# A two-layer decoder trunk on one core: x rows, early products and subtractions between the layers

## The chip, the cores and the metric

The kernel runs on one core of one Trainium2 chip. Its time is the device time of one execution in microseconds. The kernel before was timed in three runs: the median is 1912.34 us, the lowest 1910.25, the highest 1913.97. The engines named below are TensorE (PE, matmuls; PEld its weight loads), VectorE (DVE), ScalarE (ACT), GpSimd (POOL) and SyncE (SP), which issues all the transfers that matter here.

## What is computed

A trunk of two layers over 1024 rows of width 1024. Each layer adds the normalised result of a mixer to x; layer 0 mixes by a gated MLP, layer 1 by dilated attention.

```python
for i in range(DEPTH):                 # DEPTH = 2
    h = rms_norm(x, norm_pre[i])
    if i % 2 == 0:
        y = gmlp_mixer(h, ...)         # ends with y @ w_out
    else:
        y = dilated_attention_mixer(h, ...)   # begins with h @ w_in: q, k, v of 3 groups, and z
    x = x + rms_norm(y, norm_post[i])
```

All is float32. The change lies between the end of the first layer (`y @ w_out`, the addition to x) and the beginning of the second (`rms_norm` and `h @ w_in`).

## The kernel before

**Products.** Each float32 operand is split into a high and a low part (`split`: a cast on ScalarE, a subtraction on VectorE, names with hi/lo, h/l), and each product step is three matmuls (`mm3`, lines 82 to 84). The projections of layer B go by Strassen's scheme: the activations (operands `b_hi`/`b_lo` 1 to 7) and the weights (`whi`/`wlo` 1 to 7) are added up to seven pairs, and seven products of half size take the place of eight. A `Chunk` is one such projection: bv00 is the values of the first group and heads, bqk000 and bqk001 are two of queries and keys. One product is 12 matmuls of 128x512. Products 1 and 2 need no sums, only the plain upper row half's operands and one plain quarter of the weight. The weights of a chunk come in four loads (`wb0`, `wb2`, `wb1`, `wb3`, 256 KB each) into a ring of five buffers ("wraw"); four sums on POOL (`sums`, line 90) make the others: t1 from b12 and b11, t2 from b22 and t1, b12 anew, and t4. A later chunk's load goes into a buffer only when its earlier reader is done.

**The end of layer A.** `wout_unit` multiplies by w_out (accumulators `po`): loads `wr` and `yr`, their splits `oh`/`ol` and `yh`/`yl`, 16 steps. Row tiles 0, 1, 4, 5 are done first, then `post` of these four, then 2, 3, 6, 7, and `post(6)` and `post(7)` last. `post(t)` is a chain: mean square `ms_pa` on VectorE, its power −1/2 `rstd_pa` on POOL (line 105), x loaded to `xr`, `xr` = yt·rstd + xr in two halves on VectorE (line 580), stored to `x1d`; then the same norm for layer B: squares `jk_b` on ScalarE, `ms_b`, `rstd_b` on POOL, `yt` = xr·rstd·g1b in two halves on VectorE (line 154). Then the rows are brought into operands: `put_top` for tiles 0 to 3, and for 4 to 7 `put_rest`, which makes a sum and three differences with the rows of the tile 4 below, one difference on VectorE and two on POOL. Each operand is four transposes on TensorE (`pt_b`, line 128), a cast on ScalarE and a subtraction on VectorE. `yt` and `xr` share one ring "wk" of nine buffers.

**What sets the order.** Each engine runs its own queue in order. Up to the first products of layer B a scheduler sets the order by priorities and its own estimate of times; behind these the order of TensorE is written out: `in_turn` makes a list of tasks (chunk, product), `pipeline` loads weights ahead, and `drive` goes through the list and puts attention work, entered with `later(work, wait)`, between the matmuls after so many ticks (a tick is one step of three matmuls). The attention's first matmuls are the scores `s` (line 765) from K and Q, which come by 16 transfers out of the tiles `b_c`. The accumulators have tags: "mm" three banks, "o" one bank.

Of the kernel before, what the change touches and what calls it, by code (L numbers as in the profile page):

```python
# [15 lines left out]
P = 128  # L16
# [8 lines left out]
WAIT = 16  # L25
SOON = 300
SLOW = 4
RATE3 = 0.16
# [5 lines left out]
def trunk_kernel(  # L34
# [99 lines left out]

    def put_rest(pool, ops, h0, h1, t, name, first):

        a11, a12, a21, a22 = h0[:, 0:512], h0[:, 512:1024], h1[:, 0:512], h1[:, 512:1024]
        s1 = pool.tile([P, 512], F32, tag="sums", bufs=2, name=f"sums_{name}")
        add(s1, a21, a22)
        sub(a21, a11, a21, first)  # L140
        sub(a11, s1, a11, nc.gpsimd)
        sub(a12, a12, a11, nc.gpsimd)
        for i, a in ((4, a22), (5, s1), (7, a21), (6, a11), (3, a12)):
            put_op(ops, i, a, t, name)
# [133 lines left out]
    def in_turn(chunks, early=False, banks=5):  # L278

        out, n = [], 0
        if early:
            a, b = chunks[:2]
            out = [(a, 1), (a, 2), (b, 1), (b, 2), (a, 6), (a, 5), (a, 7), (b, 6), (a, 4)]
            out += [(a, 3), (b, 5), (b, 7)] if banks == 3 else [(b, 5), (a, 3), (b, 7)]
            n = 2
        for c, last in zip(chunks[n:], [chunks[n - 1] if n else None, *chunks[n:]]):
            if banks == 3:
                out += [(c, 1), (last, 4), (last, 3), (c, 6), (c, 2), (c, 5), (c, 7)]  # L290
            else:
                out += [(c, 1), (last, 4), (c, 2), (last, 3), (c, 6), (c, 5), (c, 7)]
        out += [(chunks[-1], 4), (chunks[-1], 3)]
        return [(c, i) for c, i in out if c]
# [237 lines left out]

    WK = 9
    bops = new_ops("b")
    with ExitStack() as octx:
        op = octx.enter_context(tc.tile_pool(name="op", bufs=1, reuse_waits="tile"))
        gpb = op.tile([P, D], F32, name="gpb")
        nc.sync.dma_start(out=gpb, in_=gpost[0].partition_broadcast(P))
        g1b = op.tile([P, D], F32, name="g1b")
        nc.sync.dma_start(out=g1b, in_=gpre[1].partition_broadcast(P))  # L540
# [3 lines left out]
        def wout_unit(tiles, dh):  # L544
# [6 lines left out]
            for t in tiles:  # L551
                turn[0] = (turn[0] + 1) % 4
                po[t] = psum("mm" if turn[0] else "o", [P, 512], f"po_{dh}_{t}")
                if t not in yts:
                    yts[t] = op.tile([P, D], F32, tag="wk", bufs=WK, name=f"yt_{t}")
                    sq2[t] = op.tile([P, 2], F32, tag="sq2", bufs=8, name=f"sq2_{t}")
# [18 lines left out]
        def post(t):  # L575
            r = rstd_of(op, sq2[t], f"pa_{t}")
            xt = op.tile([P, D], F32, tag="wk", bufs=WK, name=f"xr_{t}")
            nc.sync.dma_start(out=xt, in_=x[t * P:(t + 1) * P, :])
            for hs_ in HALVES:
# [6 lines left out]
            else:  # L586
                put_rest(op, bops, hs[t - 4], hs[t], t - 4, f"b{t - 4}", nc.vector)

# [71 lines left out]
    def v_chunk(q, g):  # L660
# [20 lines left out]

        return proj_t(wb[q * 10 + g * 3], bops, newb, f"bv{q}{g}", lambda th, ct, o: None, out=out, done=done)

    def qk_chunk(q, g, pr):
# [23 lines left out]
        def done():  # L708
            later(lambda: attention(q, g, pr), WAIT)
            if (q, g, pr) == (3, 2, 1):  # L710
                rate[0] = RATE3

        return proj_t(wb[q * 10 + g * 3 + 1 + pr], bops, newb, f"bqk{nm}", qk_out, done=done)

    def z_chunk(q):
# [13 lines left out]

        return proj_t(wb[q * 10 + 9], bops, newb, f"bz{q}", z_out, hooks={i: lambda c=c: prep(c) for c, i in enumerate((2, 5, 7, 4))} if q == 3 else None)  # L730

    merged, through = set(), set()
# [220 lines left out]
    side = deque()  # L953
    credit, rate = [0.5], [RATE]
    now = [0]
# [72 lines left out]
    tasks = in_turn(chunks, True, 3)  # L1028
    run(pipeline(tasks[:4], 3, tasks[4:]))
    with tc.manual_schedule(engines={mybir.EngineType.PE}):  # L1030
        drive(pipeline(tasks[4:], 3))

# [146 lines left out]
```

## Time and profile before

| | |
|---|---|
| median of three runs | 1912.34 us |
| the profiled execution's own time | 1916.06 us |
| its span, first to last instruction | 1914.3 us |
| mean granted clock of TensorE | 0.987 |
| busy: PE / DVE / ACT / POOL | 1836.5 / 1302.0 / 1002.8 / 486.1 us |
| DMA | 242.22 MB, mean 127 GB/s |

Times in the rows below are in us from the span's start. The change touches the stretch from about 620 to 820 us. Layer A's out projection ends at 739, layer B's products run from there to the end.

### The profile page before, as it was taken

The page shows a single profiled execution, that of the slowest core. Times are in us where ns is not written, and L with a number is a line of the kernel's source. Part 1 is how long each engine was busy: PE and PEld are TensorE (multiplying, and loading weights), DVE is VectorE, ACT ScalarE, POOL GpSimd, SP SyncE. Part 2 cuts the span into 40 slices and gives each one's busy share as a digit, 9 for nine tenths or more (in the row PEclk, how much of TensorE's full clock was granted, in tenths as well). Part 3 has the DMA queues.
Part 4 walks back from the last instruction along what each step waited for, and adds up shares of the span by engine and source line. Part 5 has one row for each costly group of instructions (what it writes and reads, how often), then busy time and mean ns, then how long its engine had stood idle before and what let it go on. Part 6 is the DMA issues. An engine that isn't in the chain of part 4 may idle for free.

```text
span 1914.3 us, 29722 instructions
## 1 busy us (share of the span) xinstructions
PE 1836.5 (96%) x10024; PEld 1507.9 (79%) x10024; DVE 1302.0 (68%) x2530; ACT 1002.8 (52%) x2280; POOL 486.1 (25%) x359
## 2 busy tenths in 40 slices
PE   6899999999999897999999999999999999999998
PEld 6899888888888675777778777788777787778777
DVE  6855766576555877558587685669684866868583
ACT  6544455555644665355554457464556444555931
POOL 3331343443300204222213123321233221222100
PEclk9999999999999999999999999999999998999999
DMA  6242433433256575232233554334644335433873
GB/s 209 87 129 82 140 123 114 138 118 96 78 186 232 164 248 183 67 84 74 80 82 88 156 146 119 71 86 125 165 107 105 78 90 156 130 85 74 247 208 110
DMA packets 231847, 242.22 MB, mean 127 GB/s; under 512 B 98448, under 2 KB 150288, under 8 KB 231696
## 3 DMA queue, kind: packets, MB, share of 16 engines
q1 hardware_dynamic: 231696, 240.34, 43.4%
q8 instruction: 79, 1.29, 0.3%
q14 instruction: 72, 0.59, 0.1%
HBM read 170.46 MB, written 44.63 MB: 112 GB/s over the span
## 4 chain that ended last, share of the span: by engine, by line
PE 69%; DVE 11%; DMA 7%; issue 4%; ACT 2%; SPq 2%; POOL 1%; DVEq 0%; POOLq 0%; ACTq 0%
PE p_bqk L82 6%; PE p_bqk L83 5%; PE p_bqk L84 5%; PE p_bv L82 4%; PE p_bv L83 3%; PE p_bv L84 3%; PE s L765 3%; PE po L814 3%; PE p_z L82 3%; PE p_z L84 3%; PE p_z L83 2%; PE p_u L82 2%; PE p_u L83 2%; PE p_u L84 2%; PE pT L798 2%
## 5 line engine op out<-in xcount | busy, mean ns | idle before, releaser
L82 PE MATMUL p_bqk<-b_hi,whi_bqk 128*128 128x512 f32 x672 | 269.8, 401 | 1.6 <-ACT b_x_bqk L239 1.5
L83 PE MATMUL p_bqk<-b_lo,whi_bqk 128*128 128x512 f32 x672 | 262.7, 391 | 0.0
L84 PE MATMUL p_bqk<-b_hi,wlo_bqk 128*128 128x512 f32 x672 | 262.6, 391 | 0.0
L776 ACT ACTIVATE St<-St,st 128x128 f32<-128x128 f32 (+1 forms) x384 | 168.4, 440 | 157.5 <-DVE st L773 155.4
L82 PEld LDWEIGHTS p_bqk<-b_hi,whi_bqk 128*128 128x128 f32 x672 | 126.9, 189 | 41.9 <-issue 10.8
L82 PE MATMUL p_bv<-b_hi,whi_bv 128*128 128x512 f32 x336 | 138.3, 412 | 11.2 <-DVE vt L87 10.0
L84 PEld LDWEIGHTS p_bqk<-b_hi,wlo_bqk 128*128 128x128 f32 x672 | 126.6, 188 | 27.0
L83 PEld LDWEIGHTS p_bqk<-b_lo,whi_bqk 128*128 128x128 f32 x672 | 126.9, 189 | 24.4
L84 PE MATMUL p_bv<-b_hi,wlo_bv 128*128 128x512 f32 x336 | 134.5, 400 | 0.0
L83 PE MATMUL p_bv<-b_lo,whi_bv 128*128 128x512 f32 x336 | 134.4, 400 | 0.0
L773 DVE CUSTOM_DVE_ANT_0 St<-s,mask 128x128 f32<-128x128 f32 (+1 forms) x384 | 110.6, 348 | 31.8 <-PE s L765 31.7
L83 PE MATMUL p_v<-wlo_v,a_hi 128*128 128x256 f32 x448 | 128.3, 287 | 3.9 <-DVE wlo_v L90 3.9
L84 PE MATMUL p_v<-whi_v,a_lo 128*128 128x256 f32 x448 | 128.2, 287 | 3.6 <-DVE sqa L367 2.2
L82 PE MATMUL p_v<-whi_v,a_hi 128*128 128x256 f32 x448 | 128.5, 287 | 2.9 <-DVE v_s_v L87 2.2
L90 POOL TENSOR_TENSOR wt_bqk<-wb_bqk,wt_bqk 128x512 f32<-128x512 f32 x48 | 73.7, 1536 | 193.0 <-DMA wb_bqk<-in_wb_dram 152.9
L90 DVE TENSOR_TENSOR wlo_bqk<-wb_bqk,whi_bqk 128x512 fp32r<-128x512 f32 x96 | 78.9, 822 | 57.0 <-ACT whi_bqk L96 56.3
L96 ACT CAST whi_bqk<-wb_bqk 128x512 fp32r<-128x512 f32 x96 | 59.4, 619 | 110.7 <-PE p_bqk L83 66.0
L84 PE MATMUL po<-oh,yl 128*128 128x512 f32 x256 | 100.7, 398 | 3.5 <-DVE yl L90 3.5
L83 PE MATMUL po<-ol,yh 128*128 128x512 f32 x256 | 100.6, 396 | 1.2 <-DVE ol L90 1.2
L82 PE MATMUL po<-oh,yh 128*128 128x512 f32 x256 | 101.4, 397 | 0.4 <-ACT yh L96 0.4
L90 POOL TENSOR_TENSOR wt_bqk<-wb_bqk,wb_bqk 128x512 f32<-128x512 f32 x24 | 35.1, 1463 | 249.0 <-DMA wb_bqk<-in_wb_dram 170.4
L765 PE MATMUL s<-K,Q 64*128 64x128 f32 (+1 forms) x768 | 87.5, 347 | 7.1 <-DMA K<-b_c 4.7
(262 smaller groups left out, 4820.2 us busy)
## 6 DMA issues: line engine op xcount, KB each, us to landing
wb_bqk<-in_wb_dram SPq DMA_DIRECT2D x96, 256.0 KB, 3.5
wr<-in_woa_dram SPq DMA_DIRECT2D x80, 256.0 KB, 3.6
yr<-yad SPq DMA_DIRECT2D x48, 256.0 KB, 3.4
wb_bv<-in_wb_dram SPq DMA_DIRECT2D x48, 256.0 KB, 3.1
Q<-b_c SPq DMA_DIRECT2D x192, 64.0 KB, 2.2
K<-b_c SPq DMA_DIRECT2D x192, 64.0 KB, 2.1
mo<-od SPq DMA_DIRECT2D x36, 256.0 KB, 3.6
mw<-wd SPq DMA_DIRECT2D x72, 128.0 KB, 3.5
```

The costliest lines, as they stand in the source:

```text
L82: nc.tensor.matmul(out=pso, lhsT=l_hi, rhs=r_hi, start=start, stop=False, skip_group_check=chained)
L83: nc.tensor.matmul(out=pso, lhsT=l_hi, rhs=r_lo, start=False, stop=False, skip_group_check=chained)
L84: nc.tensor.matmul(out=pso, lhsT=l_lo, rhs=r_hi, start=False, stop=stop, skip_group_check=chained)
L90: (eng or nc.vector).tensor_tensor(out=out, in0=a, in1=b, op=ALU.subtract)
L96: nc.scalar.copy(out=hi, in_=src)
L765: nc.tensor.matmul(out=pss[hh][:, cs].rearrange("p (n l) -> p n l", l=k_.shape[2]), lhsT=q_, rhs=k_, start=True, stop=True)
L773: nc.vector.tensor_tensor_reduce(out=self.S[hh][:, cs], in0=pss[hh][:, cs], in1=mk, scale=-0.125, scalar=3.0e38, op0=ALU.add, op1=ALU.min, ...
L776: nc.scalar.activation(out=self.S[hh][:, cs], in_=self.S[hh][:, cs], func=AF.Exp, scale=-1.0, bias=m, accum_out=z)
L798: nc.tensor.transpose(out=pT[hh][:, k, :], in_=self.S[hh][:, k * P:k * P + P], identity=ident)
L814: nc.tensor.matmul(out=po[64 * hh:64 * hh + 64, o:o + m * P], lhsT=V[:, kb, hh, :], rhs=self.PT[:, hh, k:k + m, :].rearrange("p k i -> p ( ...
```

## The change

It has three parts.

The x rows of `post` get a ring of their own ("xr", four buffers), and the ring "wk" goes from nine to five. The load of x row 0 is written ahead of the out projection. As the buffers allow it, the loads of rows 2, 3, 6 and 7 stand earlier in SP's queue: each waits for the store of the row that held its buffer.

In `put_rest` both the difference a21 and the difference a11 are made on VectorE, and a12 stays on POOL. The operands are made in the order 5, 6, 7, 4, 3.

Three chunks (before two) begin early, each with products 1 and 2, for which their weight quarters are loaded by themselves (`only`, names `we`), six loads, ahead of the four full ones; these six tasks carry a priority of 600 in the scheduler. Their second products are accumulated in the bank "o". The written order begins behind the six tasks, the credit of the attention work begins at 0 and the first attention unit waits 4 ticks less.

```diff
-    def put_rest(pool, ops, h0, h1, t, name, first):
+    def put_rest(pool, ops, h0, h1, t, name):
...
-        sub(a21, a11, a21, first)
-        sub(a11, s1, a11, nc.gpsimd)
+        sub(a21, a11, a21)
+        sub(a11, s1, a11)
         sub(a12, a12, a11, nc.gpsimd)
-        for i, a in ((4, a22), (5, s1), (7, a21), (6, a11), (3, a12)):
+        for i, a in ((5, s1), (6, a11), (7, a21), (4, a22), (3, a12)):
...
-            a, b = chunks[:2]
-            out = [(a, 1), (a, 2), (b, 1), (b, 2), (a, 6), (a, 5), (a, 7), (b, 6), (a, 4)]
-            out += [(a, 3), (b, 5), (b, 7)] if banks == 3 else [(b, 5), (a, 3), (b, 7)]
-            n = 2
+            a, b, c = chunks[:3]
+            out = [(d, i) for d in (a, b, c) for i in (1, 2)]
+            out += [(a, 5), (a, 6), (a, 7), (b, 6), (a, 4), (a, 3), (b, 5), (b, 7), (c, 6), (b, 4), (b, 3), (c, 5), (c, 7)]
+            n = 3
...
+        def load_x(t):
+            xts[t] = op.tile([P, D], F32, tag="xr", bufs=4, name=f"xr_{t}")
+            nc.sync.dma_start(out=xts[t], in_=x[t * P:(t + 1) * P, :])
+
+        load_x(0)
...
-                    yts[t] = op.tile([P, D], F32, tag="wk", bufs=WK, name=f"yt_{t}")
+                    yts[t] = op.tile([P, D], F32, tag="wk", bufs=5, name=f"yt_{t}")
...
-            xt = op.tile([P, D], F32, tag="wk", bufs=WK, name=f"xr_{t}")
-            nc.sync.dma_start(out=xt, in_=x[t * P:(t + 1) * P, :])
+            if t:
+                load_x(t)
+            xt = xts[t]
...
+    EARLY_TAGS = {"v": ("mm", "o", "o"), "qk": ("mm", "o", "mm")}
...
-            later(lambda: attention(q, g, pr), WAIT)
+            later(lambda: attention(q, g, pr), WAIT if q + g + pr else WAIT - 4)
...
-    credit, rate = [0.5], [RATE]
+    credit, rate = [0.0], [RATE]
...
-    run(pipeline(tasks[:4], 3, tasks[4:]))
+    for c, i in tasks[:4]:
+        c.early(i)
+    for n, (c, i) in enumerate(tasks[:6]):
+        with tc.high_priority(FIRST):
+            run(c.run(i))
+        if n < 2:
+            tasks[n + 4][0].early(tasks[n + 4][1])
+        elif n < 4:
+            tasks[n + 4][0].prep(tasks[n + 4][1])
     with tc.manual_schedule(engines={mybir.EngineType.PE}):
-        drive(pipeline(tasks[4:], 3))
+        drive(pipeline(tasks[6:], 3))
```

Three places of the queues show what it moves. The first is TensorE at the last step of the out projection (`po` of tiles 6 and 7, step 15). Before, bv00's first product (`p00_bv00`) begins behind it:

```order
L82 MATMUL po_1_7_6965<-oh_1_6_2_15_7238,yh_1_6_2_15_7244 128x512
L83 MATMUL po_1_7_6965<-ol_1_6_2_15_7239,yh_1_6_2_15_7244 128x512
L84 MATMUL po_1_7_6965<-oh_1_6_2_15_7238,yl_1_6_2_15_7245 128x512
L82 MATMUL p00_bv00_7444<-b_hi1_5163,whi1_bv00_7413 128x512
L83 MATMUL p00_bv00_7444<-b_lo1_5164,whi1_bv00_7413 128x512
```

In the changed kernel bqk001's first product (`p00_bqk0_0_1`) and bv00's second (`p10_bv00`) stand there:

```order
L84 MATMUL po_1_7_6965<-ol_1_6_2_15_7239,yh_1_6_2_15_7244 128x512
L85 MATMUL po_1_7_6965<-oh_1_6_2_15_7238,yl_1_6_2_15_7245 128x512
L83 MATMUL p00_bqk0_0_1_7519<-b_hi1_5163,whi1_bqk0_0_1_7439 128x512
L84 MATMUL p00_bqk0_0_1_7519<-b_lo1_5164,whi1_bqk0_0_1_7439 128x512
L85 MATMUL p00_bqk0_0_1_7519<-b_hi1_5163,wlo1_bqk0_0_1_7440 128x512
L83 MATMUL p00_bqk0_0_1_7519<-b_hi1_5163,whi1_bqk0_0_1_7439 128x512
L83 MATMUL p10_bv00_7443<-b_hi2_5165,whi2_bv00_7406 128x512
```

The first products of bv00 and bqk000 have moved ahead of it, among the out projection's last steps, and 24 matmuls stand between the last `po` and the ten groups of transposes.

The second is POOL in the same stretch, from the sums of bv00's weights to tile 7's `rstd_b7`. Before:

```order
L90 TENSOR_TENSOR wt1_bv00_7406<-wb1_bv00_7402,wb0_bv00_7398 128x512
L90 TENSOR_TENSOR wt2_bv00_7407<-wb3_bv00_7404,wt1_bv00_7406 128x512
L90 TENSOR_TENSOR wb1_bv00_7402<-wb3_bv00_7404,wb1_bv00_7402 128x512
L90 TENSOR_TENSOR wt4_bv00_7408<-wb2_bv00_7400,wt2_bv00_7407 128x512
L105 TENSOR_TENSOR rstd_pa_6_7263<-ms_pa_6_7260,nhalf_74 128x1
L90 TENSOR_TENSOR wt1_bqk0_0_0_7429<-wb1_bqk0_0_0_7425,wb0_bqk0_0_0_7421 128x512
L105 TENSOR_TENSOR rstd_b6_7278<-ms_b6_7275,nhalf_74 128x1
L105 TENSOR_TENSOR rstd_pa_7_7325<-ms_pa_7_7322,nhalf_74 128x1
L90 TENSOR_TENSOR wb1_bqk0_0_0_7425<-wb3_bqk0_0_0_7427,wb1_bqk0_0_0_7425 128x512
L90 TENSOR_TENSOR yt_2_6189<-sums_b2_7282,yt_2_6189 128x512
L90 TENSOR_TENSOR yt_2_6189<-yt_2_6189 128x512
L105 TENSOR_TENSOR rstd_b7_7340<-ms_b7_7337,nhalf_74 128x1
```

In the changed kernel:

```order
L106 TENSOR_TENSOR rstd_pa_6_7263<-ms_pa_6_7260,nhalf_74 128x1
L91 TENSOR_TENSOR wt1_bv00_7487<-wb1_bv00_7483,wb0_bv00_7479 128x512
L91 TENSOR_TENSOR wt2_bv00_7488<-wb3_bv00_7485,wt1_bv00_7487 128x512
L91 TENSOR_TENSOR wb1_bv00_7483<-wb3_bv00_7485,wb1_bv00_7483 128x512
L91 TENSOR_TENSOR wt4_bv00_7489<-wb2_bv00_7481,wt2_bv00_7488 128x512
L106 TENSOR_TENSOR rstd_b6_7278<-ms_b6_7275,nhalf_74 128x1
L106 TENSOR_TENSOR rstd_pa_7_7325<-ms_pa_7_7322,nhalf_74 128x1
L91 TENSOR_TENSOR wt1_bqk0_0_0_7565<-wb1_bqk0_0_0_7561,wb0_bqk0_0_0_7557 128x512
L91 TENSOR_TENSOR yt_2_6189<-yt_2_6189 128x512
L91 TENSOR_TENSOR wb1_bqk0_0_0_7561<-wb3_bqk0_0_0_7563,wb1_bqk0_0_0_7561 128x512
L91 TENSOR_TENSOR wt2_bqk0_0_0_7566<-wb3_bqk0_0_0_7563,wt1_bqk0_0_0_7565 128x512
L106 TENSOR_TENSOR rstd_b7_7340<-ms_b7_7337,nhalf_74 128x1
```

`rstd_pa_6` has moved from behind bv00's four sums to before them, `rstd_b6` now stands behind them, and tile 7's `rstd_b7` stands behind three sums of bqk000 where there were two, with one subtraction of tile 2's rows between them instead of two.

The third is SP, the stores of rows 6 and 7 and the loads of bqk000's weights. The changed kernel has here:

```order
L171 DMA wb0_bqk0_0_0_7557<-in_wb_dram 128x512
L171 DMA wb2_bqk0_0_0_7559<-in_wb_dram 128x512
L590 DMA x1d_76<-xr_6_7265 128x1024
L171 DMA wb1_bqk0_0_0_7561<-in_wb_dram 128x512
L590 DMA x1d_76<-xr_7_7327 128x1024
L171 DMA wb3_bqk0_0_0_7563<-in_wb_dram 128x512
```

The kernel before had `wb1` ahead of row 6's store and `wb3` between the two stores; both have moved behind one store more. `wb1` goes into a buffer that the last of bv00's sums on POOL (`wt4_bv00`) frees, and `wb3` into one that the first of bqk000's (`wt1_bqk0_0_0`) frees.

## Rows read from the trace of the kernel before

**Rows 1.** Totals of one engine: busy us, share of the span, instructions.

```profile
PE 1836.5 (96%) x10024; PEld 1507.9 (79%) x10024; DVE 1302.0 (68%) x2530; ACT 1002.8 (52%) x2280; POOL 486.1 (25%) x359
```

**Rows 2.** Busy time by stretch: length, engines' busy us, clock, DMA share, GB/s.

```profile
640.00:670.00 30.00, 24.93 (x127) 18.75 (x126) 27.46 (x50) 16.59 (x33) 9.82 (x9) 1.00 0.44 141
...
700.00:739.00 39.00, 35.03 (x153) 26.48 (x152) 31.45 (x65) 25.71 (x59) 4.81 (x5) 1.00 0.86 284
739.00:775.00 36.00, 25.71 (x104) 19.84 (x103) 23.33 (x41) 14.37 (x32) 16.90 (x15) 0.81 0.27 94
```

**Rows 3.** Waits of TensorE from 630 to 670: us in total, times, longest.

```profile
PE pt_b L128 <- POOL yt L90: 2.8, 4, 0.8
PE po L84 <- DVE yl L90: 1.8, 1, 1.8
```

**Rows 4.** Timeline of TensorE: start, us, instruction, idle time before and its releaser.

```profile
739.02 0.39 PE L82 MATMUL p_bv<-b_hi,whi_bv 128*128 128x512 f32 x1
...
745.60 0.39 PE L84 MATMUL p_bqk<-b_hi,wlo_bqk 128*128 128x512 f32 x1
750.09 0.95 PE L128 MATMUL pt_b<-ident,yt 128*128 128x128 f32 x4 [4.10 <-DVE yt L154]
...
760.25 0.89 PE L128 MATMUL pt_b<-ident,yt 128*128 128x128 f32 x4 [2.81 <-DVE yt L154]
...
767.14 0.80 PE L82 MATMUL p_bv<-b_hi,whi_bv 128*128 128x512 f32 x1 [1.16 <-ACT b_s_bv L239]
...
769.87 0.63 PE L82 MATMUL p_bqk<-b_hi,whi_bqk 128*128 128x512 f32 x1
```

**Rows 5.** Timeline of POOL over the step between the layers.

```profile
737.29 1.81 POOL L90 TENSOR_TENSOR wt_bv<-wb_bv,wb_bv 128x512 f32<-128x512 f32 x1 [13.22 <-DMA wb_bv<-in_wb_dram]
...
741.69 1.74 POOL L90 TENSOR_TENSOR wt_bv<-wb_bv,wt_bv 128x512 f32<-128x512 f32 x1
743.39 0.54 POOL L105 TENSOR_TENSOR rstd_pa<-ms_pa,nhalf 128x1 f32<-128x1 f32 x1
...
747.94 0.55 POOL L105 TENSOR_TENSOR rstd_b<-ms_b,nhalf 128x1 f32<-128x1 f32 x1
...
751.18 2.43 POOL L90 TENSOR_TENSOR wb_bqk<-wb_bqk,wb_bqk 128x512 f32<-128x512 f32 x1 [2.17 <-DMA wb_bqk<-in_wb_dram]
...
756.70 0.54 POOL L105 TENSOR_TENSOR rstd_b<-ms_b,nhalf 128x1 f32<-128x1 f32 x1
```

**Rows 6.** Timeline of VectorE in the same stretch.

```profile
741.01 0.14 DVE L103 TENSOR_SCALAR ms_pa<-ms_pa 128x1 f32<-128x1 f32 x1
741.07 1.20 DVE L90 TENSOR_TENSOR wlo_bqk<-wb_bqk,whi_bqk 128x512 fp32r<-128x512 f32 x1
```

**Rows 7.** Timeline of SP: the load that POOL's sum at 751.18 waits for.

```profile
748.01 0.33 SPq L170 DMA_DIRECT2D wb_bqk<-in_wb_dram  x1
```

**Rows 8.** Forms on tile `yt`, 600 to 775: min/median/max ns, first and last start.

```profile
L90 DVE TENSOR_TENSOR yt<-yt,yt x4: 682/685/691, 644.5 to 761.3; 128x512 f32<-128x512 f32 x4
L90 POOL TENSOR_TENSOR yt<-sums_b,yt x4: 1273/1280/1288, 645.4 to 762.2; 128x512 f32<-128x512 f32 x4
```

**Rows 9.** Transfers issued from 690 to 775: size of one, median us to landing.

```profile
xr<-in_x_dram SPq DMA_DIRECT2D x3, 512.0 KB, 4.2
```

**Rows 10.** Timeline of ScalarE: casts of bv00's early weights.

```profile
735.90 1.31 ACT L96 CAST whi_bv<-wb_bv 128x512 fp32r<-128x512 f32 x2
```

**Rows 11.** Timeline of TensorE at the first attention scores.

```profile
814.01 0.46 PE L765 MATMUL s<-K,Q 64*128 64x128 f32 x2 [0.48 <-DMA K<-b_c]
815.13 0.89 PE L765 MATMUL s<-K,Q 64*128 64x128 f32 x6 [0.66 <-DMA K<-b_c]
```

**Rows 12.** Timeline of SP: the first and the last of sixteen transfers of Q, K.

```profile
801.88 0.61 SPq L705 DMA_DIRECT2D Q<-b_c  x1
...
813.00 0.59 SPq L706 DMA_DIRECT2D K<-b_c  x1
```

More of the change, by code (lines that the diff above doesn't have):

```diff
@@ L26 @@
 SOON = 300
+FIRST = 600
 SLOW = 4
@@ L531, in trunk_kernel @@
         run(pipeline(in_turn([c for g in range(NG) for c in uz_chunks(g)]), 3))
-    WK = 9
     bops = new_ops("b")
@@ L538, in trunk_kernel @@
         nc.sync.dma_start(out=gpb, in_=gpost[0].partition_broadcast(P))
+        xts = {}
+        def load_x(t):
+            xts[t] = op.tile([P, D], F32, tag="xr", bufs=4, name=f"xr_{t}")
+            nc.sync.dma_start(out=xts[t], in_=x[t * P:(t + 1) * P, :])
+        load_x(0)
         g1b = op.tile([P, D], F32, name="g1b")
@@ L586, in post @@
             else:
-                put_rest(op, bops, hs[t - 4], hs[t], t - 4, f"b{t - 4}", nc.vector)
+                put_rest(op, bops, hs[t - 4], hs[t], t - 4, f"b{t - 4}")
         wout_unit((0, 1, 4, 5), 0)
@@ L680, in done @@
             later(turned(0), 4)
-        return proj_t(wb[q * 10 + g * 3], bops, newb, f"bv{q}{g}", lambda th, ct, o: None, out=out, done=done)
+        return proj_t(wb[q * 10 + g * 3], bops, newb, f"bv{q}{g}", lambda th, ct, o: None, EARLY_TAGS["v"] if q == g == 0 else ("mm",) * 3, out=out, done=done)
     def qk_chunk(q, g, pr):
@@ L708, in done @@
         def done():
-            later(lambda: attention(q, g, pr), WAIT)
+            later(lambda: attention(q, g, pr), WAIT if q + g + pr else WAIT - 4)
             if (q, g, pr) == (3, 2, 1):
                 rate[0] = RATE3
-        return proj_t(wb[q * 10 + g * 3 + 1 + pr], bops, newb, f"bqk{nm}", qk_out, done=done)
+        return proj_t(wb[q * 10 + g * 3 + 1 + pr], bops, newb, f"bqk{nm}", qk_out, EARLY_TAGS["qk"] if q == g == 0 else ("mm",) * 3, done=done)
     def z_chunk(q):
```

## Prediction

> **What bounds the kernel now.** I read the totals per engine first: TensorE is busy for 96% of the span [rows 1], so a change gains only what it takes out of TensorE's gaps, and it loses whatever it adds to them. The second view, busy time by stretch, says where the gaps are [rows 2]. The 30 us from 640 to 670 hold 5.07 us of idle TensorE, the 39 us from 700 to 739 hold 3.97 us, and the 36 us from 739 to 775, the step from one layer to the next, hold 10.29 us at a mean granted clock of 0.81. That is 19.3 us out of 1914.3; stretches in the two layers' middles run without gaps, and the change leaves their work alone. The third view, waits, names the releasers. In the first stretch they are the subtractions of `put_rest` that run on POOL (2.8 us) and one late `yl` (1.8 us) [rows 3].
>
> In the last stretch the TensorE timeline shows the chain [rows 4]. The products placed behind the last out projection begin at 739.02 and are used up at 745.60 (30 matmuls in 6.58 us, a pitch of 0.23 us). TensorE then stands still for 4.10 us until tile 6's normalised rows are there, for 2.81 us until tile 7's are (760.25), and for 1.16 us until a copy is done, and the first product behind the transposes starts at 767.14. Six of its matmuls take 2.73 us up to 769.87, 0.455 us each: the lower of the two clock levels (1.2 against 2.4 GHz), which TensorE was granted after these gaps.
>
> POOL's timeline tells why the rows are late [rows 5]. Its queue runs in order. Four weight sums of bv00 run from 737.29 to 743.43, so `rstd_pa` of tile 6 starts at 743.39, though its input on VectorE was done at 741.15 [rows 6]: 2.2 us lost. Tile 6's `rstd_b` follows at 747.94. Then one sum of bqk000 waits for its weight load, which SP issues at 748.01 and which is there at 751.18 [rows 5, 7], 3.2 us, and only behind it tile 7's `rstd_b` runs at 756.70.
>
> **The change, part by part.** Against the profiled execution (own time 1916.06 us, span 1914.3, so 1.8 us lie outside the span); the median of the runs is 1912.34, 3.7 us less, and I carry the difference over to the median.
>
> *(a) Subtractions on VectorE.* One of the two POOL subtractions of each of the four row pairs moves. On POOL it takes 1.28 us, on VectorE the like takes 0.69 [rows 8]. The second stays on POOL, so of its waits (2.8 us over four) about half goes in the first stretch, and the other half stays as a hop to POOL. The late `yl` (1.8 us) goes as well: in the new order VectorE makes the `yl` and `ol` of the next steps some 3 to 5 us sooner there, but an `ol` further on comes some 1.1 us late when the same queue is gone through in its new order with the durations it had. Gain 1.4 + 1.8 − 1.1 = 2.1 us, bounds 0 (the queue order only moves the wait) and 4.6 (both waits in full).
>
> Here a row speaks against the move. On VectorE a `wlo` of the usual 0.69 us took 1.20 us at 741.07, with a POOL sum running from 741.69 [rows 5, 6], so 0.5 us was lost beside POOL. The Trainium skill (SBUF — State Buffer, "Who interferes with whom") says that a VectorE instruction with two SBUF inputs and a POOL instruction that reads SBUF lock each other out for a whole instruction; the row agrees, and by that rule all four moved subtractions could pay. In the sum I take 0 for it: in the new order POOL's next work behind each of the moved ones waits for that very subtraction, or for a load. Its bound is 4 × 0.5 = 2 us.
>
> *(b) The x rows' own place.* Four 512 KB loads of x (three of them inside 690 to 775 us, 4.2 us to landing each [rows 9]) move from the stretch 700 to 739, where the DMA engines are 86% busy, to the one before 670, at 44% [rows 2]. The 3.97 us of gaps in 700 to 739 are mostly late halves of out projection operands, which wait for their loads. I take 1.5 us of it, bounds 0 (the operands are late by VectorE's own queue) and 3.5. The price is that each of the loads waits on SP for the store of the row that had its buffer, and weight loads queue behind it; in the first stretch, at 44%, that costs nothing that I can see.
>
> *(c) The early products.* bv00's and bqk000's first products (24 matmuls) move ahead of the last out projection steps. Nothing is saved by that alone: the end of the out projection moves back by 24 × 0.23 = 5.5 us, plus 0.6 for an operand that ScalarE had cast at 736.5 [rows 10] (two casts in 1.31 us from 735.90) and that the new order wants at 735.9, 6.1 in all. What covers the chain behind it is 24 matmuls (5.5 us) where there were 36 by 767.14, so at the first product behind the transposes 12 matmuls (2.8 us) more are done than before. The question is when that product starts.
>
> Tile 6: its input for `rstd_pa` is ready at 741.15 + 6.1 = 747.3 and now finds POOL free, since the four sums stand behind it: 2.2 us won. But `rstd_b` of tile 6 stands behind the same four sums, 6.1 us of them [rows 5]: 747.9 + 6.1 = 754.0, where its own chain (743.93 to 747.94 before, 4.0 us) would have let it run at 751.9. 2.1 us are lost again. Tile 7: behind its `rstd_pa` (0.55) POOL now has a sum of bqk000 whose second operand is loaded only into the slot that the fourth sum frees, at 754.0; 3.2 us later, 757.2, plus 1.3. The next sum's operand goes into the slot that this one frees: 758.5 + 3.2 = 761.7, then two sums of 1.29 and `rstd_b` of tile 7 at 764.3, done at 764.8. Before, the way from there to the next product was 767.14 − 757.24 = 9.9 us; the subtraction on VectorE takes 0.6 off it and the wait for the copy 1.2, since bqk000's second product needs only operands that are long there: 8.1. Start 772.9, less the 2.8 of more work: 770.1 against 767.14, so +3.0 us. Bounds: −2 if both loads land while other sums still run (3.2 × 2 off, less the two sums that stay ahead), +5 if a sum takes 2.43 us as the one at 751.18 did and a load 4.2.
>
> *(d) One bank.* The second products of all three chunks now share the single "o" bank. After the transposes three products use it one behind the other, and twice the next one waits for VectorE's add, 0.69 [rows 8] and a hop: +1.4, bounds 0 and 2.
>
> *(e) First attention unit.* It now stands 36 matmuls behind bqk000's last product, before 48. Even there its scores waited 0.48 + 0.66 us for K [rows 11], because sixteen transfers of Q and K go out one by one from 801.88 to 813.00 [rows 12], about 0.6 us each with one weight load between. Twelve matmuls less cover cost 2.8 us; the weight load between them is gone, 0.6 back: +2.2, bounds 0 (if what was late was only SP's queue) and 3.
>
> *(f) The rest.* Six more weight loads of 256 KB land beside work, and the low clock behind the transposes stays as it is (0.455 − 0.23 = 0.225 us on the six of rows 4 and two more, 1.8 us): 0, bounds −1.8 if the gaps become short and +1.
>
> The sum: −2.1 − 1.5 + 3.0 + 1.4 + 2.2 + 0 = +3.0 us. On the profiled execution 1916.06 + 3.0 = 1919.1, on the median 1912.34 + 3.0 = 1915.3. The five terms' bounds do not all fall on one side; I give the case itself −1 to +6.5, 1911.3 to 1918.8.
>
> **The rivals.** *Faster: the layer step closes up.* If the loads for POOL's sums of bqk000 are in their slots when the sums come to stand ahead of tile 7's `rstd_b`, its 2 × 3.2 us are gone, the step (c) gives −2 to −3, the gaps at 640 to 739 give their full 6 to 8 us and K is there in time. For it: the weight loads before came in 3 us and there is DMA room behind 739; SP has few other things to do. Against it: a load can't be issued before the POOL instruction that frees its slot, and the order puts the `rstd_b` behind it. With −2.5 for (c), −6 for (a) and (b) and +1 for (d) and (e): −7.5, 1904.8.
>
> *Slower: `rstd_b` behind two loads, nothing won ahead.* The mechanism is (c), at POOL's queue between 754 and 765, where tile 7's `rstd_b` is the last thing that all of layer B waits for. It decides as soon as one load lands more than 3.2 us behind its issue, or a sum runs beside VectorE at 1.8 us or more, as two of rows 5 do: +5 instead of +3.0. With (a) and (b) only moved (−1), (d) and (e) in full (+1.4 + 2.8): +8.2, 1920.5.
>
> *The change doesn't do what it says.* The early x rows only help where DMA ends the wait; if VectorE's queue does, (b) is 0, and the products in front only swap places: with (c) at 0 and (d), (e) at half, (a) in full, −2.1 + 1.8 = −0.3, 1912.0, no change.
>
> **How the numbers follow.** About 0.2%, 3.8 us, is what a measurement of this kernel can tell from no change. The forecast has 0.45: of that 0.29 within 3.8 us, 0.15 slower, 0.01 faster. The faster rival has 0.29 (0.27 faster, 0.02 same), the slower one 0.15 (0.13 slower, 0.02 same), the last one 0.11 (0.02 faster, 0.09 same). That makes faster 0.30, same 0.42, slower 0.28. The likeliest time is 1915.3. The range has to reach into both signs: down to the faster rival, 1904, up to the slower one's 1920.5, less than a fifth being left out beyond. The forecast's own range is 1911.3 to 1918.8.
>
> **What would show it.** (a) holds if TensorE's idle time in 640 to 670 falls from 5.07 to about 3, (b) if that of 700 to the end of the out projection falls from 3.97 to about 2.5. For (c) the last transpose should come at 770 to 772 in the clock of the profile before (less what (a) and (b) give), POOL should idle twice for a load of bqk000 ahead of tile 7's `rstd_b`, and that should run some 20 us behind the out projection's end. For (d) two waits of some 0.7 us for VectorE ahead of second products, for (e) a wait for K of 3 to 3.5 us. It would be wrong if the loads land before POOL needs them, if the sums run at another time than the order makes me think, or if the idle time goes elsewhere in layer B, whose later work shifts by one product.

## The result and the profile after

The changed kernel takes 1924.99 us (median of nine runs, 1918.33 to 1931.73); the kernel before, timed beside it, 1911.19 (nine runs, 1907.81 to 1917.45). The ratio is 1.0070, with an interval of 1.0055 to 1.0086: **13 us slower**, where +3.0 was forecast. The median lies 6.2 us above the forecast's own range (to 1918.8) and 4.5 above the range that takes in the rivals (to 1920.5). A second set of runs (e12 below) gave 1.0069 (1.0051 to 1.0087).

The profiled execution of the changed kernel took 1918.33 us, the lowest of its nine, and that of before 1916.06, above the median of its runs. The two traces therefore show only part of the difference. I read them for idle time, and take times from the runs.

Totals of the changed kernel, to be set beside [rows 1]:

```profile
span 1916.6 us, 29743 instructions
...
PE 1830.9 (96%) x10024; PEld 1502.2 (78%) x10024; DVE 1305.4 (68%) x2534; ACT 999.2 (52%) x2278; POOL 489.1 (26%) x355
```

Span less TensorE's busy time is 85.7 us; before it was 1914.3 − 1836.5 = 77.8. So TensorE idles 7.9 us more (87.8 us in the second trace, 10.0 more). Busy time by stretch (length, busy us, clock, DMA share, GB/s) says where; the out projection now ends near 734:

```profile
640.00:670.00 30.00, 27.87 (x138) 21.93 (x138) 25.94 (x48) 16.63 (x33) 4.87 (x5) 1.00 0.69 220
700.00:734.00 34.00, 31.41 (x137) 23.21 (x135) 26.04 (x56) 21.45 (x50) 3.16 (x4) 1.00 0.68 220
734.00:780.00 46.00, 29.02 (x112) 22.09 (x112) 28.61 (x47) 14.58 (x31) 16.54 (x14) 0.74 0.28 90
800.00:840.00 40.00, 36.11 (x163) 28.52 (x162) 27.03 (x50) 15.82 (x36) 10.52 (x8) 0.96 0.35 90
1780.00:1830.00 50.00, 41.28 (x221) 32.97 (x220) 23.99 (x69) 33.87 (x81) 4.97 (x4) 0.90 0.80 250
```

The kernel before, for the last three (the step is shifted by 5 us):

```profile
739.00:785.00 46.00, 35.71 (x148) 28.11 (x147) 27.65 (x47) 17.65 (x37) 19.86 (x17) 0.85 0.25 85
800.00:840.00 40.00, 38.86 (x194) 30.96 (x193) 30.90 (x61) 18.67 (x45) 10.79 (x8) 1.00 0.40 106
1780.00:1830.00 50.00, 46.39 (x273) 35.69 (x272) 27.95 (x83) 42.52 (x91) 5.12 (x4) 1.00 0.90 284
```

Against [rows 2] the first two stretches won: 2.13 us idle instead of 5.07, and 2.59 instead of 3.97. The step lost: 46 us hold 16.98 us idle, before 10.29, and the mean clock fell from 0.85 to 0.74 (0.81 in the second trace). Around the first scores 2.75 us of idle time came on top, near the 2.2 that the prediction put there. Around 1805, near the end of the kernel, 5.11 us came on top, and there the prediction put nothing.

The step in TensorE's timeline, to be set beside [rows 4]:

```profile
740.03 0.39 PE L85 MATMUL p_bqk<-b_hi,wlo_bqk 128*128 128x512 f32 x1
745.66 1.09 PE L129 MATMUL pt_b<-ident,sums_b 128*128 128x128 f32 x4 [5.24 <-DVE sums_b L88]
...
758.69 1.09 PE L129 MATMUL pt_b<-ident,sums_b 128*128 128x128 f32 x4 [7.18 <-DVE sums_b L88]
...
764.45 0.80 PE L83 MATMUL p_bqk<-b_hi,whi_bqk 128*128 128x512 f32 x1 [1.15 <-DVE vt L88]
...
769.96 0.47 PE L83 MATMUL p_bqk<-b_hi,whi_bqk 128*128 128x512 f32 x1 [0.88 <-DVE b_s_bqk L88]
...
773.82 0.50 PE L83 MATMUL p_bv<-b_hi,whi_bv 128*128 128x512 f32 x1 [0.85 <-DVE b_s_bqk L88]
...
780.52 0.50 PE L83 MATMUL p_bv<-b_hi,whi_bv 128*128 128x512 f32 x1 [0.97 <-ACT b_x_bv L240]
```

The cover is used up at 740, tile 6's rows are waited for 5.24 us and tile 7's 7.18 (before 4.10 and 2.81), and four waits of about 1 us follow. Behind the 7.18 us stand the queues of POOL (first list) and VectorE (second list), to be set beside [rows 5, 6]:

```profile
735.56 0.86 POOL L106 TENSOR_TENSOR rstd_pa<-ms_pa,nhalf 128x1 f32<-128x1 f32 x1 [21.40 <-DVE ms_pa L104]
...
742.25 0.55 POOL L106 TENSOR_TENSOR rstd_b<-ms_b,nhalf 128x1 f32<-128x1 f32 x1
...
747.47 1.65 POOL L91 TENSOR_TENSOR wt_bqk<-wb_bqk,wb_bqk 128x512 f32<-128x512 f32 x1 [4.14 <-DVE wlo_bv L91]
...
752.96 1.69 POOL L91 TENSOR_TENSOR wb_bqk<-wb_bqk,wb_bqk 128x512 f32<-128x512 f32 x1 [2.61 <-issue]
...
755.83 0.54 POOL L106 TENSOR_TENSOR rstd_b<-ms_b,nhalf 128x1 f32<-128x1 f32 x1
```

```profile
736.46 3.48 DVE L589 SCALAR_TENSOR_TENSOR xr<-yt,rstd_pa,xr 128x512 f32<-128x512 f32 x2 [0.44 <-POOL rstd_pa L106]
...
741.13 0.15 DVE L104 TENSOR_SCALAR ms_b<-ms_b 128x1 f32<-128x1 f32 x1
...
746.70 0.69 DVE L91 TENSOR_TENSOR wlo_bv<-wt_bv,whi_bv 128x512 fp32r<-128x512 f32 x1
```

Tile 7's `rstd_b` runs at 755.83, 22 us behind the out projection's end (before 17.7, 756.70 against 739.0). The two updates of tile 6's `xr` took 3.48 us instead of 1.4, beside bv00's sums on POOL. Tile 6's `ms_b` was nevertheless done at 741.28, and its `rstd_b` ran only at 742.25, behind the last of these sums. The first sum of bqk000 then waited until 747.47 for a buffer that VectorE's `wlo_bv` of 746.70 still read; its load, issued at 742.32 and at most 3.7 us on its way, was there before.

### The profile page after: what moved, and what is told of

Its sections match the earlier page's. It is cut to its first block, busy times and chain, and to the rows that moved or that the text cites. A ratio compares the mean times of both kernels' runs of the same rounds, so it can differ in the third digit from the quotient of the medians.

```text
span 1916.6 us, 29743 instructions
## 1 busy us (share of the span) xinstructions
PE 1830.9 (96%) x10024; PEld 1502.2 (78%) x10024; DVE 1305.4 (68%) x2534; ACT 999.2 (52%) x2278; POOL 489.1 (26%) x355
## 3 DMA queue, kind: packets, MB, share of 16 engines
q8 instruction: 79, 1.29, 0.3%
## 5 line engine op out<-in xcount | busy, mean ns | idle before, releaser
L91 DVE TENSOR_TENSOR wlo_bqk<-wt_bqk,whi_bqk 128x512 fp32r<-128x512 f32 x72 | 58.6, 814 | 60.1 <-ACT whi_bqk L97 48.8
```

Of the source, the lines that this page charges most:

```text
L91: (eng or nc.vector).tensor_tensor(out=out, in0=a, in1=b, op=ALU.subtract)
```

## The experiments

All were timed in five rounds beside the kernel before, and the ratios are to that kernel. The intervals reach 2 to 5 us to either side, so two experiments that lie less than some 4 us apart are not told from each other. "Idle" below is span less TensorE's busy time in the run's own trace; it was 77.8 us before, 85.7 and 87.8 in the two traces of the changed kernel. Each run also gives its mean granted clock; 0.001 of it is about 1.9 us on a span of 1910, an estimate that takes TensorE as busy all the time.

**e1: the attention's place alone, on the kernel before.**

```diff
-    credit, rate = [0.5], [RATE]
+    credit, rate = [0.0], [RATE]
```

> The kernel before with one number changed: the credit of the attention work starts at 0, so that every attention unit stands one product (12 matmuls) later among the projection's products, as it does in the changed kernel. Nothing at the step between the layers differs. Theory P (place of the attention): the 8.6 us wait of TensorE for a copy on ScalarE near 1805 us in the changed kernel, where the kernel before waits 1.1, comes from this shift alone, with the low clock that follows it; then this kernel is slower than before by 7 to 11 us (7.5 for the wait, 1 to 3 for the clock, 1.1 back since K is in time). Theory S (step between the layers): the loss of the changed kernel comes from the step; then this kernel is the same or 1 us faster.

Measured: 1.0014 (1.0002 to 1.0025), +2.7 us. The long wait did come, from this one number (waits of TensorE from 1780 to 1830: us in total, times, longest):

```profile
PE p_bz L82 <- ACT b_x_bz L239: 7.1, 1, 7.1
```

So the mechanism of theory P is right and its price wrong: the kernel pays 2.7, not 7 to 11. The shift takes other waits away: K is in time, and from 860 to 1780 us the gaps are some 4 us smaller, for one thing since TensorE's products of v wait 4.4 us in all for VectorE's `vt` and not 10.0. In all e1's trace idles 74.4 us, less than the 77.8 before. The mean granted clock of its runs is 0.9878, beside 0.9891 of the kernel before; that is about 2.5 us, an estimate, and so the 2.7 us fit lower clock rather than more idle time.

What waits there is seen in the changed kernel on TensorE, ScalarE, SP and POOL:

```profile
1814.22 0.79 PE L83 MATMUL p_bz<-b_hi,whi_bz 128*128 128x512 f32 x1 [8.62 <-ACT b_x_bz L240]
```

```profile
1799.05 0.62 ACT L97 CAST yl<-byr 128x512 fp32r<-128x512 f32 x1
1807.28 0.58 ACT L831 COPY oT<-po 128x512 f32<-128x512 f32 x1 [7.61 <-DMA od<-oT]
```

```profile
1794.68 1.35 SPq L735 DMA_DIRECT2D b_y<-ybd  x2
...
1803.11 0.32 SPq L737 DMA_DIRECT2D ybd<-b_z  x1
1804.35 0.32 SPq L737 DMA_DIRECT2D ybd<-b_x_bz  x1
1804.77 0.38 SPq L832 DMA_DIRECT2D od<-oT  x1
```

```profile
1801.80 1.28 POOL L94 TENSOR_TENSOR b_z<-b_z,b_y 128x512 f32<-128x512 f32 x1 [19.06 <-DMA b_y<-ybd]
```

ScalarE wants to copy an attention result into a buffer (`oT`, one buffer) whose store `od` stands on SP behind two stores of `ybd`. These wait for products of z with `b_y` on POOL, and the first of them starts at 1801.80, when `b_y`, whose loads SP issues from 1794.68 on, is there. The copy of `b_x_bz` that TensorE needs stands behind all this on ScalarE. One product's shift on TensorE turned ScalarE's wait for this buffer from 0.75 us into 7.61.

**e2: the attention's place undone, in the changed kernel.**

```diff
-            later(lambda: attention(q, g, pr), WAIT if q + g + pr else WAIT - 4)
+            later(lambda: attention(q, g, pr), WAIT if q + g + pr else WAIT - 8)
...
-    credit, rate = [0.0], [RATE]
+    credit, rate = [0.5], [RATE]
```

> The changed kernel with the attention's credit starting at 0.5 and the first unit waiting 8 ticks less instead of 4: all attention units stand among the products as in the kernel before, but the first scores come 24 matmuls behind the last product of bqk000 instead of 36. Theory P: the wait near 1805 us falls to about 1 us, 8 to 10 us back; the first scores wait 2.8 us longer for K (3.9 becomes 6.7), so the kernel is 4 to 8 us slower than before. Theory S: no gain at the end, 2.8 us more at the first scores, so 15 to 17 us slower than before.

Measured: 1.0052 (1.0034 to 1.0069), 3.5 us less than the changed kernel, which the intervals don't tell from none. The wait near 1805 fell to 1.4 us, K's wait grew from 3.9 to 6.4. The time, 9.9 us above the kernel before (6.5 to 13), lies between P's 4 to 8 and S's 15 to 17; S is out, P's size is not confirmed.

**e3: x rows and subtractions alone; e4: the early chunks alone.** The edits are the change's own hunks: e3 has those of the ring "xr" and of `put_rest`, e4 has all the others.

> The kernel before with the x rows' own ring and the subtractions on VectorE alone (operands in the new order), without the three early chunks; two early chunks, bank tags, credit and wait as before. The two traces put TensorE 4.8 us further ahead at the out projection's end in the changed kernel. If that gain is kept through the step between the layers: 4 to 6 us faster than before. If it is given back there (POOL's queue has tile 7's power behind a third sum of bqk000 in this order too): within 2 us of before.

Measured: 0.9973 (0.9961 to 0.9985), 5.1 us faster. The gain ahead of the step is kept by the runs; in the trace the step itself idles 12.5 us instead of 10.3, so some 2 us go there.

> The changed kernel without the x rows' own ring and with the subtractions and their order as before: only the three early chunks, their bank tags, credit 0 and the shorter first wait. If the parts add up: 13.4 + 5 = 18 us slower than before (both theories). If the early chunks only cost because the other two parts bring the power of tile 6 ahead of the sums (POOL's order differs here: tile 7's power stands behind one sum of bqk000, not three): 8 to 12 us slower.

Measured: 1.0090 (1.0071 to 1.0110), 17 us slower. −5 and +17 make +12 of the 13: the parts add up, and the whole loss is the early chunks' (with their bank tags, credit and first wait).

**e10, e11: the two halves of e3.**

> The kernel before with one part alone: the two differences on VectorE and the operands in the new order. By the traces this is the part that closes the gaps at 640 to 670 us (5.1 to 2.5 us idle): 2 to 3 us faster than before. If the x rows' ring carries the gain of both: the same as before.

> The kernel before with one part alone: the x rows' own ring of four buffers and the load of row 0 ahead, the subtractions as before. By the traces this is the part that closes the gaps at 700 to 740 us (4.0 to 1.8 us idle): 1 to 3 us faster than before. If VectorE's queue made those operands late and not their loads: the same as before.

Measured: 0.9996 (0.9983 to 1.0008) and 0.9992 (0.9982 to 1.0002). Neither is told from no change. With the subtractions alone TensorE's idle time from 640 to 700 falls from 5.1 to 2.1 us, but that from 700 to 735 is 5.0; the x rows alone leave 640 to 700 at 5.1 and bring 700 to 735 to 1.9. Together they close both. The two ratios add up to 2.3 us, e3 has 5.1; the intervals don't tell these apart.

**e5, e6: the weight sums of bv00 and bqk000 on VectorE**, e5 on top of e3, e6 in the changed kernel.

```diff
-            sub(t1, b12, b11, nc.gpsimd)
+            eng = nc.vector if self.name in ("bv00", "bqk0_0_0") else nc.gpsimd
+            sub(t1, b12, b11, eng)
...
```

> The kernel before with the x rows' ring and the subtractions on VectorE (4 us faster than before by its runs), and now also the eight weight sums of bv00 and bqk000 on VectorE instead of POOL, so that POOL's queue at the step holds only the powers and one subtraction for each row pair. Theory Q (POOL's queue sets the rows' time): the powers of tiles 6 and 7 come 2 to 5 us sooner and the step's idle time falls from 12.5 to 8 to 10 us; 6 to 9 us faster than before. Rival (VectorE pays instead: each sum takes 0.7 us in the queue that also carries the rows): no gain over the 4 us, or some lost.

Measured: 0.9979 (0.9964 to 0.9995). No gain over e3.

> The changed kernel with the eight weight sums of bv00 and bqk000 on VectorE instead of POOL. Theory Q: tile 6's two updates of x fall from 3.5 us to 1.4, since no POOL sum runs beside them, tile 7's power no longer stands behind three sums, and the wait of 7.2 us for tile 7's rows falls to 2 to 4; 5 to 8 us faster than the changed kernel, 6 to 9 us slower than before. Rival (the rows' own chain is as long without POOL): no more than 2 us off the changed kernel.

Measured: 1.0079 (1.0055 to 1.0104), nothing gained, though the trace shows the mechanism as expected: the two updates of `xr` took 1.41 us again, and the wait for tile 7's rows fell from 7.18 to 5.41. Idle time fell to 80.9 us, but in this trace busy time rose to 1838.6, from 1830.9 and 1830.0 in the two of the changed kernel, with a mean clock of 0.986: what the gaps gave back went into matmuls at the lower clock. Over the six runs the clock is 0.9867, beside 0.9871 and 0.9877 of the changed kernel, which makes 1 to 2 us of it; the rest isn't explained.

**e7: other banks, e8: no priority for the early products**, both in the changed kernel.

```diff
-            out += [(a, 5), (a, 6), (a, 7), (b, 6), (a, 4), (a, 3), (b, 5), (b, 7), (c, 6), (b, 4), (b, 3), (c, 5), (c, 7)]
+            out += [(a, 6), (a, 5), (a, 7), (b, 6), (a, 4), (a, 3), (b, 5), (b, 7), (c, 6), (b, 4), (b, 3), (c, 5), (c, 7)]
...
-        return proj_t(wb[q * 10 + g * 3 + 1 + pr], bops, newb, f"bqk{nm}", qk_out, EARLY_TAGS["qk"] if q == g == 0 else ("mm",) * 3, done=done)
+        return proj_t(wb[q * 10 + g * 3 + 1 + pr], bops, newb, f"bqk{nm}", qk_out, (("mm", "s", "mm") if pr else ("mm", "o", "mm")) if q == g == 0 else ("mm",) * 3, done=done)
...
-    EARLY_TAGS = {"v": ("mm", "o", "o"), "qk": ("mm", "o", "mm")}
+    EARLY_TAGS = {"v": ("mm", "o", "t"), "qk": ("mm", "o", "mm")}
```

> The changed kernel with two other bank tags and one swap: bqk001's second product goes to a bank of s, bv00's fifth to a bank of t (both free there, the transposes being done) instead of the single o, and bv00's product 6 comes before its 5, so that 7 doesn't follow 6 in the same bank. Theory: the four waits of 0.9 to 1.1 us behind the transposes go, 3 to 4 us faster than the changed kernel. Rival (the waits only move, since the same VectorE adds and weight casts are due there): under 1 us.

Measured: 1.0068 (1.0048 to 1.0089): under 1 us off. In the trace the four waits behind the transposes are gone, and the 46 us behind the out projection's end hold 13.7 us of idle time instead of 17.0. But one of 1.3 us for a copy of `vt` has come at 791, and in all the trace idles 87.1 us, no less than the changed kernel: what the banks give at the step is lost in other places.

```diff
-FIRST = 600
+FIRST = 0
```

> The changed kernel with the scheduler's priority of the six early tasks at 0 instead of 600: bv00's and bqk000's first products no longer go ahead of the out projection's last steps; all 48 matmuls of the four early products stand behind it, some of them between the transposes. Theory M (the early products give away their cover): the out projection ends 5 to 6 us sooner, the rows follow it, and the 5.2 and 7.2 us waits for the rows shrink by 5 us together; 4 to 7 us faster than the changed kernel. Rival (POOL's queue and the loads set the rows' time, wherever the products stand): within 2 us of the changed kernel.

Measured: 1.0065 (1.0046 to 1.0085), within 2 us, the rival's. The waits for the rows changed their names: 4.2 us for a POOL subtraction that now stands behind bv00's sums, 3.0 for tile 7. The 46 us behind the out projection's end hold 15.0 us of idle time instead of 17.0, but all of the trace 85.6, as the changed kernel.

**e12: the changed kernel again.**

> The changed kernel once more, for a second trace and beside the others on one chip. In its first trace the idle time of TensorE is 8.5 us above that of the kernel before, while its runs are 13.4 us slower. Theory L (the rest is low clock, which each longer gap brings in some executions): this trace shows the same idle time within 2 us, but more matmuls at the low clock than the first one had (about 12 us of loss there). Rival (idle time that differs from run to run makes the rest): the same loss by low clock, another idle time.

Measured: 1.0069 (1.0051 to 1.0087); the trace has 2 us more idle time than the first one and about the same low clock. Theory L is not borne out by this trace. The clocks of the runs speak for it: on this chip the six runs of the changed kernel have a mean of 0.9877, the 29 of the kernel before 0.9896. The difference is worth about 3.6 us, an estimate. With the 8 to 10 us of idle time that comes to 12 to 14.

**e9: the four edits of e2, e6, e7, e8 together.**

> The changed kernel with the four edits tried singly put together: credit 0.5 with the first unit 8 ticks earlier (attention among the products as before), priority 0 for the early tasks, the bank tags s and t with product 6 ahead of 5, and the weight sums of bv00 and bqk000 on VectorE. Theory A (the loss is a sum of separate gaps, each with its stretch of low clock, and the edits' shares add): the idle time at the step falls from 17 to about 9 us, the wait near 1805 us to about 1 us, a longer wait for K (6.4 us) stays; 8 to 12 us faster than the changed kernel, that is 1 to 5 us slower than before. Rival B (the three early chunks cost wherever their gaps are closed, since the same rows end last): no better than the best of the single edits, 9 to 12 us slower than before.

Measured: 0.9983 (0.9972 to 0.9993): 16 us faster than the changed kernel, 3 faster than before, more than theory A gave. The edits had given 3.5, nothing, under 1 and 1 us singly. That sums to some 3 us, about 10 either way since four intervals add up; 16 lies outside. At the step the longest waits that are left are these (waits of TensorE, 600 to 870; K's is the price of the earlier first unit):

```profile
PE s L778 <- DMA K<-b_c: 6.9, 2, 6.4
PE pt_b L129 <- DVE sums_b L88: 5.3, 4, 3.7
```

The reading is that the edits at the step work on one chain: 48 matmuls behind the out projection cover it only if POOL's sums don't stand in it, and the sums matter only once the products do. e13 and e14 below take two of the four edits back; the priority and the banks were not taken back singly, so some 11 of the 16 us are not split between these two and their working together.

**e13, e14: e9 with one edit taken back**, the attention's place (e13) and the weight sums (e14).

> All edits of e9 but the attention's place: credit 0 and the first unit 4 ticks earlier, as in the changed kernel. Theory P2 (the place of the attention costs by the wait near 1805 us, whatever the step does): that wait is back at 6 to 9 us, with 2 to 3 us of low clock behind it, and K waits 2.8 us less; 5 to 8 us slower than e9, 2 to 5 slower than before. Rival (single edits only work together, so each taken out costs most of the 16): 10 us or more slower than e9.

Measured: 0.9988 (0.9974 to 1.0002), 1 us slower than e9, which is not told from none. The wait near 1805 is back (7.2 us) and K's fell from 6.9 to 3.9. So by their ratios the shift costs 1 to 3.5 us net in e1, e2 and e13, of which e1's alone is clear of noise; in e2 and e13 the net has a wait for K that is 2.5 to 3 us longer on the other side, since the first unit's wait changes with the credit.

> All edits of e9 but the weight sums, which are on POOL again as in the changed kernel. Theory Q2 (POOL's queue sets the rows' time once the early products stand behind the out projection): the idle time at the step rises from 4.4 to 8 to 11 us; 5 to 8 us slower than e9. Rival (VectorE's sums were not needed): within 2 us of e9.

Measured: 1.0007 (0.9998 to 1.0017), 4.6 us slower than e9. On this base POOL's queue is worth what theory Q2 said, nearly (waits of TensorE, 600 to 870):

```profile
PE pt_b L129 <- POOL yt L91: 5.9, 4, 4.2
```

**e15, e16: bqk000 ends sooner**, e15 in e9 (with the first unit's wait 4 ticks shorter than before, and `(a, 6)` ahead of `(a, 5)` as in e9), e16 in the changed kernel. The edit of e16:

```diff
-            out += [(a, 5), (a, 6), (a, 7), (b, 6), (a, 4), (a, 3), (b, 5), (b, 7), (c, 6), (b, 4), (b, 3), (c, 5), (c, 7)]
+            out += [(a, 5), (a, 6), (a, 7), (b, 6), (a, 4), (b, 5), (b, 7), (a, 3), (b, 4), (b, 3), (c, 6), (c, 5), (c, 7)]
```

> All edits of e9, and the task list with bqk000's last products ahead of bqk001's product 6, so that the first scores stand 36 matmuls behind bqk000's end (24 in e9), with the first unit's wait 4 ticks shorter than before instead of 8. Theory E (each 12 matmuls less of cover cost 2.8 us in the wait for K): that wait falls from 6.9 to about 4 us; 2.5 to 4 us faster than e9, 5 to 7 us faster than before. Rival (the wait moves to the weights or the accumulators of the moved products): within 1.5 us of e9.

Measured: **0.9946 (0.9933 to 0.9958), 10 us faster than before**, 1898.7 us, 7 faster than e9. It beats both kernels. K's wait fell from 6.9 to 2.1 us, and the stretch around it, 780 to 860, which e9 ran at a mean clock of 0.94, runs at full clock (waits of TensorE, then busy time of that stretch):

```profile
PE s L778 <- DMA K<-b_c: 2.1, 2, 1.1
```

```profile
780.00:860.00 80.00, 77.90 (x424) 61.84 (x422) 50.94 (x103) 41.18 (x102) 20.59 (x14) 1.00 0.28 80
```

> The changed kernel with the task list alone changed: bqk000's last products come ahead of bqk001's product 6, so that the first scores, at the same place as in the changed kernel, stand 48 matmuls behind bqk000's end instead of 36. Theory E (cover of the wait for K): the wait of 3.9 us falls to about 1 us and the low clock near 820 us goes; 3 to 6 us faster than the changed kernel. Rival (a single edit's gain is lost again to another wait, as with the sums and the banks): under 2 us.

Measured: 1.0051 (1.0039 to 1.0064), 3.5 us off the changed kernel. Of the single edits this one alone has a gain that is clear of noise, and only just; the wait for K does not appear among TensorE's waits from 800 to 870 any more, only the 2.2 us for `vt`.

## Why the prediction was wrong, step by step

**The gain ahead of the step** was right: (a) and (b) were put at 2.1 + 1.5 = 3.6 us, and e3 measured 5.1 (2.9 to 7.4). The traces give 2.9 us in 640 to 670 and 1.4 in 700 to the end of the out projection. Whether the two pay more together than singly is not shown (e10, e11).

**What failed is the price of the early chunks.** The terms (c) to (f) were put at 3.0 + 1.4 + 2.2 + 0 = +6.6 us; e4 measured 17 (13.6 to 21). Their upper bounds, 5 + 2 + 3 + 1, make 11, so these were too narrow as well. The next paragraphs take the terms one by one.

**The contention in (a)** was put at 0 for the moved subtractions, and that holds: they took 0.69 us in the changed kernel too. But the row that spoke of it [rows 5, 6] was weighed for the wrong instructions. In the new order `rstd_pa` comes ahead of bv00's sums, so the updates of `xr`, which wait for it, start together with these sums: 3.48 us (3.54 in e12) where e6, with the sums off POOL, has 1.41. The Trainium skill (SBUF — State Buffer, "Who interferes with whom") has the rule that fits: a VectorE instruction with two SBUF inputs and a POOL instruction that reads SBUF exclude each other for a whole instruction. The trace agrees: 2 us are lost on VectorE. On the path that ended last they are not seen in full, since tile 6's `ms_b` was done 1 us before POOL came to its `rstd_b`.

**The step (c)** had the right chain and was too small. Tile 7's `rstd_b` was to run 19 us behind the out projection's end and ran 22 us behind. Of the 3 us between, 2 lie in one wait. POOL's two waits for bqk000 were both taken for weight loads of 3.2 us. From tile 6's `rstd_b` (742.25) to bqk000's first sum (747.47) it was 5.2 us, because that sum writes into a `wt` buffer (a ring of three) that VectorE's `wlo_bv` held: it stood in VectorE's queue behind tile 6's `yt` and tile 7's updates. The ring of the loads was worked out, the ring of the sums was not. The rest is the second load (3.8 us from the end of the first sum to the next instead of 3.2) and sums of 1.65 and 1.69 us instead of 1.29. The idle time of the step, out projection's end to 780, rose by 6.7 us; (c) and (d) together were put at 4.4.

**The bank (d)** was put at two waits, 1.4 us. There were three (1.15, 0.88, 0.85) and a fourth (0.97) from product 7 right behind 6 in one bank, as the task list of the diff has them. That is 3.9 us in the trace; what they cost in time is not shown, since e7 gave under 1.

**The first scores (e)** were put at +2.2; the wait for K is 3.9 us, +2.8, as the mechanism said. The price of a wait was taken as the wait itself. In e16 that fits, 3.9 us less wait gave 3.5 us. In e15 4.8 us less gave 7.1 (some 3 either way), and in its trace the lower clock behind the gap went as well; that the price is above the wait is not clear of noise.

**The low clock (f)** was put at 0, because the gaps were thought to stay as they were. They grew, and the granted clock of the step fell from 0.85 to 0.74 (0.81 in e12's trace), that around the scores from 1.00 to 0.96, that near 1805 from 1.00 to 0.90. Over the whole span the two first traces have the same clock (0.987 before, 0.988 after), so they don't show its price; the runs of e12 put it at about 3.6 us, an estimate.

**The term without a price** is the sentence that the layers' middles run without gaps and that the change leaves their work alone. The three stretches that the prediction read hold 19.3 of the 77.8 us of idle time; 58.5 lay elsewhere, 19.8 of it between 860 and 1780. The prediction names the shift by one product only among the signs of being wrong, and no term has it. No wait behind the first scores was looked at for what a shift does to it, and the one near 1805 went from 1.1 to 8.6 us. By e1, e2 and e13 the shift costs 1 to 3.5 us net. So it is the smaller part of the missing 10 us. The larger part lies at the step: e13, which leaves the shift in and has the three edits there, is 15 us faster than the changed kernel.

**The rivals.** The slower one named POOL's queue at tile 7's `rstd_b`, with 1920.5. That is where the step's largest wait is, but taking POOL's sums away alone gave nothing (e6), and on e9's ground they cost 4.6 us (e14); so it is one of several and not the deciding mechanism. "The change doesn't do what it says" is out: the x rows' part works and the products stand where they were to stand. The range ended at 1920.5, the slower rival's time. The bounds of the single terms were not added up, though (c) at its upper bound, (d), (e) and the clock all point the same way and hang on the same gaps; added up, with nothing won ahead, they reach 1923.3, still under the measured time.

What stays open: how the loss at the step splits between the early products' place, POOL's queue and the banks, since the priority and the banks were not taken back singly in e9, and why e6's shorter gaps don't show in its runs. For the banks and the priority (e7, e8) the traces agree with the runs: in all they idle as long as the changed kernel.

## What to carry to other kernels

Work that is moved from behind the start of a serial chain to a place ahead of it no longer covers that chain: count what stands behind the chain's start, not what is done sooner. (Here that is a reading of the traces; e8, which moved the work back alone, gained 1 us, not told from none.) When an order is shifted by one task, look at every wait of the rest of the kernel that has less than a task's slack, to the last microsecond, and look at the granted clock behind each gap too. Edits can be worth 3 us when their single gains are added and 16 us together, so a single edit without effect doesn't clear its cause. And look at every ring of buffers that a queue writes to, not only at those that its loads fill.

## What the runs showed of the hardware

The updates of `xr`, with both tensor operands in SBUF, took up to 1.78 us each beside POOL's sums, 0.74 alone. The clock's part differs from one execution to the next: TensorE's busy time for the same number of matmuls was between 1826.7 (e15, mean clock 0.994) and 1840.9 us (e4, 0.984).
